# Feed-forward units of seven products: deferring the seventh, exchanging the fifth and sixth

## The chip, the cores and the metric

The kernel runs on one core of a Trainium2 chip. The metric is device time in microseconds for one execution, taken over several executions; the median of the runs is used. A profile of one execution gives each engine's instructions with their times. Engines: TensorE (PE) multiplies, ScalarE (ACT), VectorE (DVE) and GpSimd (POOL) work on tiles, SyncE (SP) issues the transfers.

## The reference

One decoder block on x of 2048 positions by 1024 channels, float32, batch 1:

```
h  = rmsnorm(x); z = h @ w_in                    # one combined input projection
a  = gated linear attention on part of z          # 4 heads, in chunks of 64
b  = B * conv3(C * h') on the rest of z           # causal, width 3
x1 = x + concat(a, b) @ w_out
f  = rmsnorm(x1); y = x1 + (silu(f @ w_gate) * (f @ w_up)) @ w_down   # D_FF = 2816
out = rmsnorm(y)
```

The change concerns the last matrix products, those with w_gate, w_up and w_down.

## The kernel before, in words

Tensors lie with channels on the 128 partitions and positions in the free dimension, in blocks of 512 positions (PB). The positions are worked on in two halves of two blocks each.

**A unit.** Every large product is cut into units. A unit multiplies a 2x2 arrangement of weight blocks by a 2x2 arrangement of operand blocks with seven products in place of eight (PRODUCTS, L36 to 39): A11·B11, S1·T1, S2·T2, A12·B21, S3·T3, S4·B22, A22·T4. The S are sums of weight blocks, made on POOL in `unit_weights` (L424 to 441: L430, L431, L432, and L437 for S4's, which overwrites A12's raw block). The T are sums of operand blocks, made ahead. A product adds the partial products of its blocks of 128 channels in one PSUM bank; it is 12 matmuls in the input projection and in the gate and up products (four blocks), 9 in most down products (three), 6 in the first group of them (two). Each block takes three matmuls (`product_step`, L443 to 450), since weights and operands are split into a high and a low part: `split` (L162) rounds with ACT (L163) and subtracts with DVE (L164). Split weights lie in a pool of four buffers (`wqp`), split operands in a pool of 28 (`opp`).

**Evacuation.** The seven products of a unit use two banks, `oa` and `ob` (L483 to 497). A11 goes to `oa`, which ACT copies to c11 (L480); S1 goes to `ob`, copied to c22; S2 is accumulated on top of A11 in `oa`, copied to c12; A12 goes to a bank of its own and DVE adds it to c11 (`plus`, L472 to 473); S3 is accumulated in `oa`, which DVE adds to c22; S4 is accumulated in `ob`, which DVE adds to c12; A22 is accumulated in `oa`, which is c21. So S2 may begin when c11 is copied, S3 when c12 is copied, S4 when c22 is copied, and A22 when `oa` has been added to c22. In down units of a later group the copies are DVE adds onto the running sums y (`onto`); in the first group they are ACT copies to y (`into`).

**Feed-forward.** `ffn_up` (L1048) goes through 11 pairs of units for each half: an even unit gives gate values, which ACT puts through silu (L512), an odd unit gives the factor, which DVE multiplies in (L1054). POOL then makes T1 to T4 for the down product (L1058), and `split_later` (L1065) splits and stores them in the background. `ffn_down` (L1083) takes them in groups starting at 0, 2, 5 and 8 (GROUPS), four units in each. The last unit of half 1 is `last_unit` (L1162). `load_pairs` (L662) and `load_h2` (L1039) load a whole half's operands; LATER (L42) is the order in which `h2_rest` (L995) splits the later operands of half 0.

**Work beside it.** During half 0's first units `h2_ahead` (L1022) prepares half 1's operands: `position_rstd` (L187) sums squares with small matmuls (`rs`, L196), does Newton steps on tiles of 128x4 on DVE (L200, L213 to 218), spreads the result (`rep`, L204) and turns it with PE (`rb_ps`, L208). `finish_later` does the like for the final norm of half 0's output during half 1.

**What sets the order.** The whole kernel is one program in a tile framework that tracks the readiness of tiles and is asked to schedule by a simulated timeline (L1383). The order in which an engine gets its instructions is that scheduler's. The source order is a priority, `issue_after` and `behind` (L155) add constraints, and each engine then runs its own stream in order.

Of the kernel before, what the change touches and what calls it, by code (L numbers as in the profile page):

```python
# [19 lines left out]
P = 128  # L20
D = 1024
SEQ = 2048
PB = 512
# [17 lines left out]

LATER = ("B21", "T3", "B22", "T4")  # L42

# [9 lines left out]
def tile_hymba_block(ctx, tc, x, xt, win, wa, wgu, wout, wffn, wdown, wdown_first, small, out):  # L53
# [93 lines left out]
    def store(dst, src):  # L147
        return nc.sync.dma_start(dst, src)
# [274 lines left out]

    def unit_weights(src, raw=None):  # L424
        raw = raw_weights(src) if raw is None else raw
        n = src.shape[-1]
        a11, a12, a22, a21 = [raw[:, i, :] for i in range(4)]
        s1 = rawp.tile([P, PB], F32, name="s1", tag="s1", bufs=1)[:, 0:n]
        w = {"A11": weight_quarter(a11)}
        pool.tensor_tensor(s1, a21, a22, ALU.add)  # L430
        pool.tensor_tensor(a21, a11, a21, ALU.subtract)  # L431
        pool.tensor_tensor(a11, s1, a11, ALU.subtract)  # L432
        w["S1"] = weight_quarter(s1)
        w["S2"] = weight_quarter(a11)
        w["A12"] = weight_quarter(a12)
        w["S3"] = weight_quarter(a21)
        pool.tensor_tensor(a12, a12, a11, ALU.subtract)  # L437
# [13 lines left out]

    def unit(src, ops, into=None, onto=None, raw=None):

        w = unit_weights(src, raw)
        unit_splits[:] = last_hi + last_lo
# [4 lines left out]

        def mul(i, o=None):
            first = o is None
            o = bank() if first else o
            n, m = PRODUCTS[i]
# [9 lines left out]
        def copied(name, o, at):  # L476
# [4 lines left out]
            return t  # L481


        oa = mul(0)
        c11 = copied("c11", oa, (0, 0))
        ob = mul(1)
# [12 lines left out]

# [162 lines left out]
    def load_pairs(src):  # L662
        ops = no_operands()
        for _, n in PRODUCTS:
            ops[n] = [(load_whole if n in WHOLE else load_pair)(p) for p in src[n]]
        return ops

    def load_whole(src):
# [80 lines left out]
    def in_proj(half, ops, first=None, differences=None):  # L749
        def units():  # L750
            for u in range(12):
                with ExitStack() as stack:
                    if half == 0 and u == 1:
                        stack.enter_context(tc.issue_after(last_load[0].ins))
                    if half or u > 1:
                        us = unit(win[u], ops)
                    else:
                        us = plain_unit(win[u], ops, differences) if u else first
                if half == 0 and u == 1:
                    del ops["B12"]  # L760
                    differences(("T4",))
                yield us

        units = units()
        for dst, i0 in ((s_kq, 0), (s_kq, 2), (s_v, 0), (s_v, 2)):
            for r, j, c, p in next(units):
                store(dst[2 * half + j][i0 + r][:], settled(c, p)[:])
        for i0 in (0, 2):
            for r, j, c, p in next(units):
                store(s_g[2 * half + j][i0 + r][:], silu(c, p)[:])  # L770
        background.append(gla_half(half))
        for i0 in (0, 2):
            cc = {(r, j): settled(c, p) for r, j, c, p in next(units)}
            ch = {(r, j): c for r, j, c, _ in next(units)}
            for r in range(2):
                i = i0 + r
                left = halo[:, i, :]
                for j in range(2):
                    s = tp.tile([P, PB + 2], F32, name="u", tag="t")
                    dve.tensor_tensor(s[:, 2:], ch[r, j][:], cc[r, j][:], ALU.mult)  # L780
                    act.activation(s[:, 0:2], left, AF.Copy)
                    left = s[:, PB : PB + 2]
                    y = cc[r, j]
                    act.activation(y[:], s[:, 0:PB], AF.Copy, scale=col(C_CW + i))
                    for n in (1, 2):
                        dve.scalar_tensor_tensor(
                            y[:], s[:, n : n + PB], col(C_CW + 4 * n + i), y[:], ALU.mult, ALU.add
                        )
                if half == 0:
                    act.activation(halo[:, i, :], left, AF.Copy)  # L790
            for r, j, c, _ in next(units):
                y = cc[r, j]
# [5 lines left out]
                store(dst[:, 1, :], y[:])  # L798


    def gla_half(half):
# [237 lines left out]
    def load_h2():  # L1039
        ops, loads = no_operands(), raw_loads[-2]  # L1040
        for _, n in PRODUCTS:
            for k in range(4):
                with tc.issue_after(loads.ins):
                    o = (load_whole if n in WHOLE else load_pair)(s_h2p[n][k])
                ops[n].append(o)
        return ops

    def ffn_up(half, ops):  # L1048
        for m in range(NF // 2):
            us = unit(wffn[2 * m], ops)  # L1050
            sg = {(r, j): silu(c, p) for r, j, c, p in us}
            for r, j, c, _ in unit(wffn[2 * m + 1], ops):
                s = sg[r, j]
                dve.tensor_tensor(s[:], c[:], s[:], ALU.mult)  # L1054
            b11, b12, b21, b22 = [sg[r, j] for r in range(2) for j in range(2)]
            t1, t2, t3, t4 = [bt(n) for n in ("t1", "t2", "t3", "t4")]
            for y, p, q in ((t1, b12, b11), (t2, b22, t1), (t3, b22, b12), (t4, b21, t2)):
                pool.tensor_tensor(y[:], p[:], q[:], ALU.subtract)  # L1058
            values = [("B11", b11), ("B21", b21), ("B22", b22)]
            if half == 1 and m >= LAST_GROUP:  # L1060
                values.append(("B12", b12))
            values += [("T1", t1), ("T2", t2), ("T3", t3), ("T4", t4)]
            background.insert(0, split_later(s_act[half][m], values))

# [15 lines left out]
    def act_op(half, m, n):  # L1080
        return (load_whole if n in WHOLE else load_pair)(s_act[half][m][n])

    def ffn_down(half):  # L1083

# [5 lines left out]
        for u, m0 in enumerate(GROUPS):  # L1090
            ms = range(m0, m0 + (3 if u else 2))
            last = m0 == LAST_GROUP
            if last:
                drain_background()
            raw = None
            if u:
                raw = raw_weights(wdown[4 * u - 4])
                with tc.issue_after(raw_loads[-1].ins):
                    ops = {n: [group_op(m, n) for m in ms] for _, n in PRODUCTS}
            else:  # L1100
                ops = {n: [group_op(m, n) for m in ms] for _, n in PRODUCTS}
            if last and half:
# [4 lines left out]
            for d0 in range(0, KD, 2):  # L1107
                src = wdown[4 * u - 4 + d0 // 2] if u else wdown_first[d0 // 2]
                if u == 0 and d0 == 2:

                    order = [(m, n) for _, n in PRODUCTS for m in range(GROUPS[1], GROUPS[2])]
                    for m, n in order[:EARLY]:
                        early[m, n] = act_op(half, m, n)
                if u == 0:
                    for d in (d0, d0 + 1):
                        if d < KD - 1:
                            pair = opp.tile([P, 2, PB], F32, name="y", tag="op")
                        for j in range(2):
                            y[d, j] = pair[:, j, :] if d < KD - 1 else bt("y")[:]
                    unit(src, ops, {(r, j): y[d0 + r, j] for r in range(2) for j in range(2)})  # L1120
                    continue
                xs = []
                if u < 3:
                    for d in (d0, d0 + 1):
                        xs.append((y[d, u - 1], bt("x1")))
                        load(xs[-1][1][:], s_x1[2 * half + u - 1][d][:])
# [4 lines left out]
                unit(src, ops, onto=onto, raw=None if d0 else raw)  # L1131
                for r, j in ((0, 0), (1, 1), (0, 1), (1, 0)):
                    yy = onto[r, j]
# [3 lines left out]
                    elif last:  # L1137
                        store(s_x1[2 * half + j][d0 + r][:], yy)
                for yy, x1 in xs:
                    pool.tensor_tensor(yy, x1[:], yy, ALU.add)  # L1140
        if half == 0:
# [246 lines left out]
```

## Time and profile before

| quantity | value |
|---|---|
| median of 3 runs | 2062.14 us (2060.34 to 2063.09) |
| span of the profiled execution | 2059.3 us (its own time is not listed apart from it) |
| PE busy | 2018.4 us, 98% |
| DVE, ACT, POOL busy | 69%, 47%, 42% |
| mean granted TensorE clock | 0.996 |

The input projection and the mixers run up to some 570 us, the output projection and what belongs to it up to some 760 us, the feed-forward part from there to the end. In the rows of a timeline or a group, a line such as L473 is that of the kernel before; the name before the arrow is the tile written, the names behind it are those read, with buffer numbers left out; a bracket holds the idle time of the engine ahead of the instruction and what ended it.

### The profile page before, as it was taken

The page shows a single profiled execution, that of the slowest core. Times are in us where ns is not written, and L with a number is a line of the kernel's source. Part 1 is how long each engine was busy: PE and PEld are TensorE (multiplying, and loading weights), DVE is VectorE, ACT ScalarE, POOL GpSimd, SP SyncE. Part 2 cuts the span into 40 slices and gives each one's busy share as a digit, 9 for nine tenths or more (in the row PEclk, how much of TensorE's full clock was granted, in tenths as well). Part 3 has the DMA queues.
Part 4 walks back from the last instruction along what each step waited for, and adds up shares of the span by engine and source line. Part 5 has one row for each costly group of instructions (what it writes and reads, how often), then busy time and mean ns, then how long its engine had stood idle before and what let it go on. Part 6 is the DMA issues. An engine that isn't in the chain of part 4 may idle for free.

```text
span 2059.3 us, 27063 instructions
## 1 busy us (share of the span) xinstructions
PE 2018.4 (98%) x9229; PEld 1657.3 (80%) x9229; DVE 1425.3 (69%) x2128; ACT 959.7 (47%) x1918; POOL 859.8 (42%) x622
## 2 busy tenths in 40 slices
PE   7999999999999999999999999999999999999997
PEld 6877888787888888888888878787888888878786
DVE  8789686559743886676675676767666666667774
ACT  6655365765542344444444452334434444453344
POOL 0345322122102564464564345534644544435544
PEclk9999999999999999999999999999999999999998
DMA  6378485416586873545454676476444434586653
GB/s 229 116 274 278 159 319 165 143 67 194 190 296 246 311 254 130 198 181 207 156 185 143 241 264 254 185 282 257 163 164 167 175 140 169 179 309 223 234 217 126
DMA packets 188729, 421.47 MB, mean 205 GB/s; under 512 B 19792, under 2 KB 65072, under 8 KB 178992
## 3 DMA queue, kind: packets, MB, share of 16 engines
q1 hardware_dynamic: 188592, 419.76, 57.2%
q8 instruction: 72, 1.18, 0.2%
q14 instruction: 65, 0.53, 0.1%
HBM read 274.98 MB, written 144.70 MB: 204 GB/s over the span
## 4 chain that ended last, share of the span: by engine, by line
PE 84%; DVE 7%; DMA 4%; ACT 3%; issue 1%; POOL 1%; SPq 0%; DVEq 0%; ACTq 0%; POOLq 0%
PE mm L448 24%; PE mm L449 23%; PE mm L450 23%; PE mm L945 3%; PE mm L948 3%; PE mm L946 3%; DVE wq L164 2%; DVE op L164 1%; DMA op<-sa_B 1%; DMA op<-sa_T 1%; PE a_ps L702 1%; ACT wq L163 1%; DMA siT<-lo 1%; PE o_ps L869 1%; PE o_ps L871 1%
## 5 line engine op out<-in xcount | busy, mean ns | idle before, releaser
L448 PE MATMUL mm<-op,wq 128*128 128x512 f32 x2499 | 973.7, 392 | 10.3 <-ACT c L480 5.3
L449 PE MATMUL mm<-op,wq 128*128 128x512 f32 x2499 | 972.5, 390 | 1.6 <-DVE op L164 1.6
L450 PE MATMUL mm<-op,wq 128*128 128x512 f32 x2499 | 961.3, 390 | 2.6 <-DVE wq L164 2.3
L164 DVE TENSOR_TENSOR wq<-raw,wq 128x512 fp32r<-128x512 f32 (+2 forms) x626 | 508.9, 818 | 262.6 <-ACT wq L163 260.0
L163 ACT ACTIVATE wq<-raw 128x512 fp32r<-128x512 f32 (+2 forms) x626 | 364.9, 589 | 585.6 <-PE mm L450 447.9
L448 PEld LDWEIGHTS mm<-op,wq 128*128 128x128 f32 x2499 | 468.9, 188 | 114.9 <-ACT c L480 8.0
L450 PEld LDWEIGHTS mm<-op,wq 128*128 128x128 f32 x2499 | 469.1, 188 | 103.8 <-DVE wq L164 6.1
L449 PEld LDWEIGHTS mm<-op,wq 128*128 128x128 f32 x2499 | 469.3, 188 | 99.1 <-DVE op L164 3.7
L432 POOL TENSOR_TENSOR raw<-s,raw 128x512 f32<-128x512 f32 (+2 forms) x97 | 133.3, 1374 | 518.5 <-DVE wq L164 474.7
L430 POOL TENSOR_TENSOR s<-raw 128x512 f32<-128x512 f32 (+2 forms) x97 | 127.4, 1313 | 247.5 <-DMA raw<-in_wffn_dram 90.7
L473 DVE TENSOR_TENSOR c<-mm,c 128x512 f32<-128x512 f32 x198 | 135.8, 686 | 72.7 <-PE mm L450 70.9
L473 DVE TENSOR_TENSOR y<-mm,y 128x512 f32<-128x512 f32 x185 | 126.9, 687 | 83.3 <-PE mm L450 82.9
L437 POOL TENSOR_TENSOR raw<-raw 128x512 f32<-128x512 f32 (+2 forms) x97 | 120.6, 1244 | 126.7 <-DVE wq L164 126.7
L927 POOL TENSOR_TENSOR ssx<-ssx,q 128x512 f32<-128x512 f32 x52 | 77.4, 1504 | 158.8 <-ACT q L926 158.5
L431 POOL TENSOR_TENSOR raw<-raw 128x512 f32<-128x512 f32 (+2 forms) x97 | 137.3, 1416 | 4.9
L480 ACT ACTIVATE c<-mm 128x512 f32<-128x512 f32 x198 | 116.1, 587 | 11.1 <-PE mm L450 9.3
L945 PE MATMUL mm<-op,wq 128*128 128x512 f32 x256 | 100.9, 395 | 0.0
L946 PE MATMUL mm<-op,wq 128*128 128x512 f32 x256 | 99.7, 389 | 0.0
L163 ACT ACTIVATE wq<-s 128x512 fp32r<-128x512 f32 (+2 forms) x97 | 56.9, 587 | 89.3 <-PE mm L450 85.4
L164 DVE TENSOR_TENSOR wq<-s,wq 128x512 fp32r<-128x512 f32 (+2 forms) x97 | 82.6, 852 | 2.8 <-ACT wq L163 2.1
L164 DVE TENSOR_TENSOR op<-op 128x512 fp32r<-128x512 f32 x94 | 76.8, 844 | 4.7 <-ACT op L163 4.6
L948 PE MATMUL mm<-op,wq 128*128 128x512 f32 x256 | 79.8, 390 | 0.0
(204 smaller groups left out, 1807.6 us busy)
## 6 DMA issues: line engine op xcount, KB each, us to landing
raw<-in_wffn_dram SPq DMA_DIRECT2D x44, 1024.0 KB, 6.5
sa_B<-so SPq DMA_DIRECT2D x47, 512.0 KB, 4.2
op<-sa_B SPq DMA_DIRECT2D x47, 512.0 KB, 7.1
raw<-in_win_dram SPq DMA_DIRECT2D x23, 1024.0 KB, 5.4
sa_T<-so SPq DMA_DIRECT2D x44, 512.0 KB, 4.5
op<-sa_T SPq DMA_DIRECT2D x44, 512.0 KB, 6.9
raw<-in_wdown_dram SPq DMA_DIRECT2D x24, 768.0 KB, 5.8
sx<-y SPq DMA_DIRECT2D x48, 256.0 KB, 4.0
```

Source lines behind the costliest of these rows:

```text
L163: last_hi[:] = [act.activation(hi, src, AF.Copy)]
L164: last_lo[:] = [dve.tensor_tensor(lo, src, hi.bitcast(F32), ALU.subtract)]
L430: pool.tensor_tensor(s1, a21, a22, ALU.add)
L431: pool.tensor_tensor(a21, a11, a21, ALU.subtract)
L432: pool.tensor_tensor(a11, s1, a11, ALU.subtract)
L448: pe.matmul(o[:], wh, xh, start=first and k == 0, stop=False, skip_group_check=True)
L449: pe.matmul(o[:], wh, xl, start=False, stop=False, skip_group_check=True)
L450: return pe.matmul(o[:], wl, xh, start=False, stop=k == n - 1, skip_group_check=True)
L473: dve.tensor_tensor(t[:], o[:], t[:], ALU.add)
L945: pe.matmul(o[e, j][:], wh, m[:, 0, :], start=k == 0, stop=False)
L946: pe.matmul(o[e, j][:], wh, m[:, 1, :], start=False, stop=False)
L948: pe.matmul(o[e, j][:], wl, ops[k][j][:, 0, :], start=False, stop=k == KD - 1)
```

## The change

In the feed-forward units the source now puts the seventh product A22 behind the next unit's A11 and S1 (`pending`, `rest`, `fourth`), and S4 ahead of S3. Each unit's weights are split in that order (S4 ahead of S3). The operands T4 of the next stage are loaded only when the deferred product has been written (`late`, `fill_now_or_late`). Since c21 now comes later, a unit no longer returns its results: it hands each to a function `use` (`gated`, `raised` in `gate_and_up`, which replaces the body of `ffn_up`). The input projection keeps its old order (`close=True`), as does the last but one down unit of half 1; `in_proj` is rewritten to the form with `use`, and the convolution becomes a function. LATER takes B22 ahead of T3, and the orders of loading take OVERLAPPED.

The core of the diff:

```diff
+OVERLAPPED = [PRODUCTS[i] for i in (0, 1, 2, 3, 5, 4, 6)]
-LATER = ("B21", "T3", "B22", "T4")
+LATER = ("B21", "B22", "T3", "T4")
...
-    def unit_weights(src, raw=None):
+    pending, late, operand = [], [], dict(PRODUCTS)
+
+    def unit_weights(src, raw, close):
...
-        w["S3"] = weight_quarter(a21)
+        if close:
+            w["S3"] = weight_quarter(a21)
         pool.tensor_tensor(a12, a12, a11, ALU.subtract)
         w["S4"] = weight_quarter(a12)
+        if not close:
+            w["S3"] = weight_quarter(a21)
         w["A22"] = weight_quarter(a22)
...
+        def rest():
+            mul("A22", oa)
+            if into is not None or onto is not None:
+                copied("c21", oa, (1, 0))
+            return oa
+
+        def fourth():
+            rest()
+            if use is not None:
+                use(1, 0, oa, True)
+
+        oa = mul("A11")
         c11 = copied("c11", oa, (0, 0))
+        ob = mul("S1")
         c22 = copied("c22", ob, (1, 1))
-        mul(2, oa)
+        if before is not None:
+            before()
+        while late:
+            late.pop(0)()
+        mul("S2", oa)
         c12 = copied("c12", oa, (0, 1))
-        plus(c11, mul(3))
-        mul(4, oa)
-        plus(c22, oa)
-        mul(5, ob)
+        plus(c11, mul("A12"))
+        if close:
+            mul("S3", oa)
+            plus(c22, oa)
+        mul("S4", ob)
         plus(c12, ob)
-        mul(6, oa)
-        if into is not None or onto is not None:
-            copied("c21", oa, (1, 0))
-        return [(0, 0, c11, False), (1, 1, c22, False), (0, 1, c12, False), (1, 0, oa, True)]
+        if not close:
+            mul("S3", oa)
+            plus(c22, oa)
+        if close:
+            rest()
+        if use is not None:
+            for r, j, c in ((0, 0, c11), (1, 1, c22), (0, 1, c12)):
+                use(r, j, c, False)
+            if close:
+                use(1, 0, oa, True)
+        if not close:
+            pending.append(fourth)
...
+    def fill_now_or_late(n, fill):
+        if n == PRODUCTS[-1][1] and pending:
+            late.append(fill)
+        else:
+            fill()
...
+                close = bool(last and half and d0 == KD - 4)
+                unit(src, ops, use, onto=onto, raw=None if d0 else raw, close=close)
```

More of the change, by code (lines that the diff above doesn't have):

```diff
@@ L450, in product_step, with unit @@
         return pe.matmul(o[:], wl, xh, start=False, stop=k == n - 1, skip_group_check=True)
-    def unit(src, ops, into=None, onto=None, raw=None):
-        w = unit_weights(src, raw)
+    def unit(src, ops, use=None, into=None, onto=None, raw=None, close=False):
+        w = unit_weights(src, raw, close)
+        before = pending.pop() if pending else None
         unit_splits[:] = last_hi + last_lo
@@ L749, in in_proj @@
     def in_proj(half, ops, first=None, differences=None):
[L750 to L767, printed above, removed]
+        count = iter(range(12))
+        def run(use):
+            u = next(count)
+            if half or u > 1:
+                unit(win[u], ops, use, close=True)
+                return
+            us = first
+            if u:
+                with tc.issue_after(last_load[0].ins):
+                    us = plain_unit(win[u], ops, differences)
+                del ops["B12"]
+                differences(("T4",))
+            for x in us:
+                use(*x)
@@ L768, in in_proj, with keep, output_gate @@
+        for s, i0 in ((s_kq, 0), (s_kq, 2), (s_v, 0), (s_v, 2)):
+            def keep(r, j, c, p, s=s, i0=i0):
+                store(s[2 * half + j][i0 + r][:], settled(c, p)[:])
+            run(keep)
         for i0 in (0, 2):
-            for r, j, c, p in next(units):
+            def output_gate(r, j, c, p, i0=i0):
                 store(s_g[2 * half + j][i0 + r][:], silu(c, p)[:])
-        background.append(gla_half(half))
+                if (i0, r, j) == (2, 1, 0):
+                    background.append(gla_half(half))
+            run(output_gate)
@@ L772, in in_proj @@
         for i0 in (0, 2):
[L773 to L790, printed above, removed]
@@ L791, in in_proj, with first_factor, second_factor, output_factor @@
-            for r, j, c, _ in next(units):
+            cc, ch = {}, {}
+            def first_factor(r, j, c, p, cc=cc):
+                cc[r, j] = settled(c, p)
+            def second_factor(r, j, c, p, cc=cc, ch=ch, i0=i0):
+                ch[r, j] = c
+                if (r, 1 - j) in ch:
+                    convolution(half, i0 + r, [ch[r, e] for e in range(2)], [cc[r, e] for e in range(2)])
+            def output_factor(r, j, c, p, cc=cc, i0=i0):
                 y = cc[r, j]
@@ L798, in in_proj, with convolution @@
                 store(dst[:, 1, :], y[:])
+            for use in (first_factor, second_factor, output_factor):
+                run(use)
+    def convolution(half, i, ch, cc):
+        left = halo[:, i, :]
+        for j in range(2):
+            s = tp.tile([P, PB + 2], F32, name="u", tag="t")
+            dve.tensor_tensor(s[:, 2:], ch[j][:], cc[j][:], ALU.mult)
+            act.activation(s[:, 0:2], left, AF.Copy)
+            left = s[:, PB : PB + 2]
+            y = cc[j]
+            act.activation(y[:], s[:, 0:PB], AF.Copy, scale=col(C_CW + i))
+            for n in (1, 2):
+                dve.scalar_tensor_tensor(
+                    y[:], s[:, n : n + PB], col(C_CW + 4 * n + i), y[:], ALU.mult, ALU.add
+                )
+        if half == 0:
+            act.activation(halo[:, i, :], left, AF.Copy)
     def gla_half(half):
@@ L1040, in load_h2, with fill @@
         ops, loads = no_operands(), raw_loads[-2]
[L1041 to L1045, printed above, removed]
+        for _, n in OVERLAPPED:
+            def fill(n=n):
+                for k in range(4):
+                    with tc.issue_after(loads.ins):
+                        o = (load_whole if n in WHOLE else load_pair)(s_h2p[n][k])
+                    ops[n].append(o)
+            fill_now_or_late(n, fill)
         return ops
@@ L1081, in act_op, with group_ops, fill @@
         return (load_whole if n in WHOLE else load_pair)(s_act[half][m][n])
+    def group_ops(ms, group_op, marks):
+        ops = no_operands()
+        for _, n in OVERLAPPED:
+            def fill(n=n):
+                with behind(marks):
+                    ops[n] += [group_op(m, n) for m in ms]
+            fill_now_or_late(n, fill)
+        return ops
     def ffn_down(half):
@@ L1094, in ffn_down @@
                 drain_background()
[L1095 to L1101, printed above, removed]
+            raw = raw_weights(wdown[4 * u - 4]) if u else None
+            ops = group_ops(ms, group_op, raw_loads[-1:] if u else [])
             if last and half:
@@ L1109, in ffn_down @@
                 if u == 0 and d0 == 2:
-                    order = [(m, n) for _, n in PRODUCTS for m in range(GROUPS[1], GROUPS[2])]
+                    order = [(m, n) for _, n in OVERLAPPED for m in range(GROUPS[1], GROUPS[2])]
                     for m, n in order[:EARLY]:
@@ L1119, in ffn_down @@
                             y[d, j] = pair[:, j, :] if d < KD - 1 else bt("y")[:]
[L1120 removed]
+                    unit(src, ops, into={(r, j): y[d0 + r, j] for r in range(2) for j in range(2)})
                     continue
[L1122 removed]
+                xs = {}
                 if u < 3:
[L1124 to L1126 removed]
+                    for r in range(2):
+                        x1 = xs[r, u - 1] = bt("x1")
+                        load(x1[:], s_x1[2 * half + u - 1][d0 + r][:])
                 if last and half and d0 == KD - 2:
@@ L1130, in ffn_down, with use @@
                 onto = {(r, j): y[d0 + r, j] for r in range(2) for j in range(2)}
-                unit(src, ops, onto=onto, raw=None if d0 else raw)
-                for r, j in ((0, 0), (1, 1), (0, 1), (1, 0)):
+                def use(r, j, *_, onto=onto, xs=xs, last=last, d0=d0):
                     yy = onto[r, j]
```

53 lines of the change are left out of this document (32 added, 21 removed).

## The prediction

> **What bounds the kernel now.** I first read the busy shares and the granted clock on the page, then the busy time by stretch from 760 us on (the feed-forward part), then the waits of PE there.
>
> ```profile
> span 2059.3 us, 27063 instructions
> PE 2018.4 (98%) x9229; PEld 1657.3 (80%) x9229; DVE 1425.3 (69%) x2128; ACT 959.7 (47%) x1918; POOL 859.8 (42%) x622
> PEclk9999999999999999999999999999999999999998
> ...
> 850.00:950.00 100.00, 100.00 (x443) 82.78 (x442) 67.50 (x86) 46.85 (x83) 48.12 (x34) 1.00 0.52 185
> ...
> 1050.00:1150.00 100.00, 100.00 (x443) 82.81 (x442) 59.62 (x75) 41.82 (x73) 49.55 (x36) 1.00 0.41 146
> ```
>
> PE is the bound. In the 300 us from 850 to 1150 (the first and last of three rows alike are shown) it is busy without a break at clock 1.00: 443 matmuls in 100 us, 0.226 us each, so a product of 12 matmuls is 2.72 us and a unit of seven 19.0 us. In such a stretch no order of products can gain anything; only a wait of PE can be taken away. These are all of PE's waits from 760 us to the end (waited for: us in total, times, longest):
>
> ```profile
> PE mm L448 <- ACT c L480: 3.5, 3, 1.7
> PE mm L448 <- DVE y L473: 3.4, 3, 1.7
> PE rb_ps L1195 <- DVE rep L1188: 1.7, 1, 1.7
> PE mm L449 <- DVE op L164: 1.6, 2, 1.4
> PE rs L1175 <- ACT q L1232: 1.4, 1, 1.4
> PE rb_ps L208 <- DVE rep L204: 0.9, 1, 0.9
> PE mm L450 <- DVE wq L164: 0.5, 2, 0.3
> PE mm L448 <- DVE c L473: 0.4, 1, 0.4
> ```
>
> They sum to 13.4 us, of which 3.1 (L1195, L1175) belong to the end of the kernel, behind the last product. So the whole feed-forward part offers about 10 us, 0.5% of the time.
>
> **What the change really moves.** The source of before runs a unit's seven products and then the next unit's. The chip does not: the kernel is built with a list scheduler (L1383), and the profile shows what that made of it. This is DVE in one up-projection unit (start us, us, engine, line):
>
> ```profile
> 911.65 0.69 DVE L473 TENSOR_TENSOR c<-mm,c 128x512 f32<-128x512 f32 x1 [0.19 <-PE mm L450]
> ...
> 914.37 0.69 DVE L473 TENSOR_TENSOR c<-mm,c 128x512 f32<-128x512 f32 x1 [0.33 <-PE mm L450]
> ...
> 922.31 0.69 DVE L1054 TENSOR_TENSOR sg<-mm,sg 128x512 f32<-128x512 f32 x1 [3.08 <-PE mm L450]
> ```
>
> The first two add the fifth and sixth products in the order run; the third reads the seventh from PSUM. It comes 922.31 − 914.37 = 7.94 us after the sixth, three products, not one: two products of the next unit already stand between. The built instruction streams say the same by name. Before runs, in its usual unit, A11', S1' (11 of 12 matmuls), A22 of the unit before, A12' and S2' mixed, S4', S3': the deferral and the exchange that the diff writes down are there. After runs A11', S1', A22, A12' and S2' mixed, S4', S3'. Both streams hold the same number of instructions on every engine and the same order on each up to about 765 us. I therefore cost the change only where the two orders differ at a wait. Below, H0u3 is unit 3 (from 0) of half 0's up-projection; even units are gates.
>
> **Removed.** Four places of before wait for an evacuation that after issues earlier, or further from its reader.
>
> ```profile
> 833.55 0.39 PE L450 MATMUL mm<-op,wq 128*128 128x512 f32 x1
> 833.95 0.63 ACT L163 ACTIVATE so<-c 128x512 fp32r<-128x512 f32 x1 [2.76 <-DVE c L1054]
> 834.49 0.58 ACT L480 ACTIVATE c<-mm 128x512 f32<-128x512 f32 x1
> 835.12 0.50 PE L448 MATMUL mm<-op,wq 128*128 128x512 f32 x1 [1.18 <-ACT c L480]
> 835.46 0.40 PE L449 MATMUL mm<-op,wq 128*128 128x512 f32 x1
> ...
> 1425.64 0.39 PE L450 MATMUL mm<-op,wq 128*128 128x512 f32 x1
> 1427.08 0.59 ACT L480 ACTIVATE c<-mm 128x512 f32<-128x512 f32 x1
> 1427.72 0.50 PE L448 MATMUL mm<-op,wq 128*128 128x512 f32 x1 [1.70 <-ACT c L480]
> ...
> 1501.31 0.95 PE L196 MATMUL rs<-ones,ssx 128*128 128x1 f32 x8
> 1502.29 0.59 ACT L480 ACTIVATE c<-mm 128x512 f32<-128x512 f32 x1
> 1502.93 0.50 PE L448 MATMUL mm<-op,wq 128*128 128x512 f32 x1 [0.67 <-ACT c L480]
> ...
> 1686.00 0.40 PE L450 MATMUL mm<-op,wq 128*128 128x512 f32 x1
> 1686.23 0.50 PE L196 MATMUL rs<-ones,ssx 128*128 128x1 f32 x4
> 1686.43 0.69 DVE L473 TENSOR_TENSOR c<-mm,c 128x512 f32<-128x512 f32 x1 [0.94 <-PE mm L450]
> 1687.18 0.50 PE L448 MATMUL mm<-op,wq 128*128 128x512 f32 x1 [0.44 <-DVE c L473]
> ```
>
> A wait costs its start-to-start time less 0.23, and 0.11 more for the matmul behind it (835.46 − 835.12 = 0.34, not 0.23).
> - H0u3, product S3: 835.12 − 833.55 − 0.23 + 0.11 = **1.45**. The copy of c12, which frees the bank, stood on ACT behind a split of `so` that waited for DVE's gate product. In after the copy is ahead of that split. What is late next is nothing nearer than the 13 matmuls between.
> - H1u1, S2: 1427.72 − 1425.64 − 0.23 + 0.11 = **1.96**, for the copy of c11. In after the first unit's products end earlier beside the second's, and the copy is issued before S1'.
> - H1u5, S2: 1502.93 − 1502.26 (the end of the eight `rs` matmuls) + 0.11 = **0.8**; in after A22 of the unit before stands between, 12 matmuls for a copy of 0.59.
> - H1u14, A22 directly behind its own S3: 0.44 + 0.11 = **0.6**, and the wait for `rep` behind it (L204, the row of 0.9 above, + 0.11) **1.0**. In after H1u15's A11 and the `rs` matmuls stand between.
>
> Sum **−5.8** (−4.3 if H0u3's stays).
>
> **Added.** In two units after puts A22 directly behind its own S3, where before had two products of the next unit between: H0u1 and H0u2. There h2_ahead's row statistics (position_rstd) stand in DVE's queue, and the next unit's weight splits with them. PE then waits for `plus(c22)`. Its floor is what H1u14 shows with an idle DVE: 1687.18 − 1686.00 − 0.23 + 0.11 = 1.06 us, twice 2.1. To it comes what is queued on DVE ahead of that add. In H0u1 this is, during S4 and S3 (5.4 us): two weight splits, one split of `so`, two gate products (L1054), the add of c12 and nine or ten Newton steps. Before runs the same kind of work a little elsewhere:
>
> ```profile
> 789.01 0.68 DVE L1054 TENSOR_TENSOR c<-c,c 128x512 f32<-128x512 f32 x1
> 789.61 0.17 DVE L213 TENSOR_SCALAR rs<-rs 128x4 int32<-128x4 int32 x1
> 789.81 0.16 DVE L214 TENSOR_SCALAR py<-rs 128x4 int32<-128x4 int32 x1
> ...
> 797.47 1.51 DVE L164 TENSOR_TENSOR wq<-raw,wq 128x512 fp32r<-128x512 f32 x1
> 798.90 1.77 DVE L1054 TENSOR_TENSOR c<-c,c 128x512 f32<-128x512 f32 x1
> ...
> L164 DVE TENSOR_TENSOR wq<-raw,wq 128x512 fp32r<-128x512 f32 x436 | 382.9, 883 | 239.7 <-ACT wq L163 237.1
> ...
> L473 DVE TENSOR_TENSOR c<-mm,c 128x512 f32<-128x512 f32 x198 | 135.8, 686 | 72.7 <-PE mm L450 70.9
> ```
>
> At 0.2 us a Newton step (789.81 − 789.61) and 0.69 the rest, that is 10 × 0.2 + 6 × 0.69 = 6.1 us in 5.4: 0.7 late. At 1.51 and 1.77 for half of the five that slow down (beside POOL) it is about 3 late. I take 0.9, near the fast rows at 789 us, as POOL mostly waits in that stretch: 2.0 for H0u1 (1.06 to 4.1). H0u2 has one split less and no gate product: 1.4 (1.06 to 3.0). `rb` (L208) then follows A22 and waits for a `rep` whose chain passes the same queue: 0.3 (0 to 1.2). Sum **+3.7** (2.1 to 8.3).
>
> A rule of the Trainium skill speaks against this place. By "SBUF — State Buffer", section "SBUF: two separate sides", a DVE instruction with two SBUF inputs and a GpSimd one that reads SBUF exclude each other for a whole instruction, whichever begins first. The trace agrees: splits and gate products (two SBUF inputs) run 0.68 or up to 1.77, the adds out of PSUM 0.686 on average over 198. By that rule, if POOL works through the whole stretch, the two waits would be the upper ends above and the sum +2.5; by what I take it is −2.1.
>
> **Costed at nothing.** The waits at the first down units (1197 and 1839 us, DVE y, 1.5 to 1.7 each), at 1289 to 1305, 1409 and 1931 to 1947 have the same queue ahead of them in both streams, so I leave them: between −1 each and +1. The S3/S4 exchange of the weights puts S4's split on ACT ahead of S3's, where it waits for POOL's L437 (rivals). T4's later loads are the same transfers on the same queue, read by the seventh product, over two products away. LATER only reorders splits. New tight places (S3 directly behind S4 in some down units; A12's split) have covers of 1.4 us against a copy of 0.59: 0 to 0.5 each, taken as 0.
>
> **Sum.** −5.8 + 3.7 = −2.1 on the profiled span: 2059.3 → 2057.2. The median of the three runs lies 2.84 above that span (the execution's own time is not given apart from it), so **2062.1 − 2.1 = 2060.0 us**.
>
> **Rivals.**
> 1. *Slower: S4's weights come late in every unit.* The chain is A12's split, L437 on POOL, S4's split, with ACT's queue held at its head meanwhile. For it: ACT waits for L437 in before already. Rows:
>
> ```profile
> ACT wq L163 <- POOL raw L437: 36.8, 21, 4.5
> ...
> L437 POOL TENSOR_TENSOR raw<-raw 128x512 f32<-128x512 f32 x66 | 89.3, 1354 | 89.8 <-DVE wq L164 89.8
> ```
>
> Against it: from the release of A12's buffer to S4's first matmul lie 49 matmuls in both streams, 11.1 us; the chain is 0.63 + 1.77 + 1.35 + 0.63 + 1.77 = 6.2, or 8.9 with two more POOL instructions of that length ahead. It decides once it passes 11.1 us. If it did so by 0.3 in each of the 44 up units: +13.2 beside the −2.1, 2073 us; from half of them on it is 2066.6, slower than before by over 0.2%.
> 2. *Faster: the written order frees more than I list.* If the waits that I left alone also go (3.4 + 1.6 + 0.5 = 5.5), or DVE is not late at H0u1 and H0u2 (2.1 in place of 3.7): −3.7 to −9, 2053 to 2058.4. For it: these waits stem from the same kind of queueing. Against: the two streams agree there.
> 3. *No change beyond noise, because the old order was already the new one.* This is my forecast; if not even the four waits go, but the added ones come, +3.7: 2066.
>
> **How the numbers follow.** A measurement of this kernel can tell about 0.2% (4.1 us) from no change: faster is under 2058.0, slower over 2066.3. Chances: the forecast 0.60 (own range 2058 to 2066), the faster rival 0.22, the slower rival with the upper ends of the added waits 0.18. So faster 0.22, same 0.60, slower 0.18. For 8 in 10 the range takes the forecast's range and the nearer part of the faster rival: 2056 to 2066.5.
>
> **What would show it right or wrong.** In the profile of after: PE's waits for ACT's c copy fall from 3.5 to under 1; a wait for DVE's c add (the line of `plus`) rises from 0.4 to 2 to 6, in two pieces between 780 and 820 us; 850 to 1150 stays at 100 busy in every 100 us; the y waits stay near 3.4. It is wrong if gaps appear in the steady stretch, above all waits for wq (rival 1), if the c-add wait stays under 1, or if the y waits go.

## The result, and the profile after

After takes 2066.47 us (median of 6 runs, 2065.95 to 2071.88), before 2061.07 (median of 6, 2059.01 to 2063.09): ratio **1.0027, 95% interval 1.0015 to 1.0039**, slower by 5.4 us. The forecast was 2060.0, 2.1 us faster than before. The time lies at the very upper end of the range, 2056 to 2066.5; the sign is wrong.

The page of after, and all of PE's waits from 760 us on (waited for: us in total, times, longest; line numbers in the rows from here on are those of the kernel they come from; in after L456 to L458 are the three matmuls of product_step, L482 is `plus`, L489 the ACT copy, L166 and L167 the two halves of `split`):

```profile
span 2065.0 us, 27060 instructions
PE 2021.9 (98%) x9229; PEld 1657.5 (80%) x9229; DVE 1401.8 (68%) x2128; ACT 959.8 (46%) x1918; POOL 861.1 (42%) x622
...
PE mm L458 <- DVE wq L167: 7.4, 10, 1.3
PE mm L456 <- DVE y L482: 2.4, 2, 1.3
PE rb_ps L1274 <- DVE rep L1267: 1.7, 1, 1.7
PE mm L456 <- DVE c L482: 1.6, 2, 0.8
PE rs L1254 <- ACT q L1311: 1.4, 1, 1.4
PE rb_ps L211 <- DVE rep L207: 1.0, 1, 1.0
```

The waits for ACT's copies of c (3.5 in before) are gone, and so are those for `op` (1.6). The two directly following seventh products show as the wait for DVE's c, 1.6. What is new and large is the first row: PE waits ten times, 7.4 us, for the low half of split weights; before had 0.5. Part of it lies where before had no gap at all (busy by stretch):

```profile
850.00:950.00 100.00, 99.60 (x439) 81.91 (x438) 61.66 (x83) 46.05 (x82) 51.15 (x36) 1.00 0.51 179
950.00:1050.00 100.00, 99.55 (x438) 81.86 (x437) 66.45 (x85) 43.80 (x77) 56.47 (x38) 1.00 0.51 180
1050.00:1150.00 100.00, 98.81 (x436) 81.38 (x435) 61.52 (x78) 43.65 (x75) 46.56 (x33) 1.00 0.44 157
```

DVE is less busy in them than before (189.6 us in 300 against 199.5), so it is no want of DVE time: the splits stand at another place in its queue.

**Where the time went.** Both kernels have the same number of product matmuls, so the n-th of one can be laid beside the n-th of the other, and the difference of their start times followed. This is by how much it grows in each stretch (us; times are those of before):

| stretch of before | forecast | after | what it is |
|---|---|---|---|
| to 774 | 0 | +1.92 | there by 600 us, where both streams are alike; see the last section |
| 774 to 820 | +3.7 | +3.39 | H0u1 and H0u2, seventh directly behind sixth |
| 820 to 838 | −1.45 | −1.40 | H0u3, copy of c12 |
| 838 to 1172 | 0 | **+3.36** | A11 of H0u7 and u11, S1 of u15 split late |
| 1172 to 1285 | 0 | −0.33 | first down groups |
| 1285 to 1405 | 0 | **+2.31** | last down group of half 0 |
| 1405 to 1440 | −1.96 | −3.31 | H1u1's c11, and the wait for `op` at 1410 |
| 1440 to 1700 | −2.4 | −2.23 | H1u5, H1u14 |
| 1700 to 2036 | 0 | **+2.02** | down units of half 1, most in the last group |

From 774 us on this is +3.8. The three bold rows, which the forecast put at nothing, are 7.7 together.

The added seventh products look as they were drawn. In H0u2 (start, us, engine, line):

```profile
821.07 0.39 PE L458 MATMUL mm<-op,wq 128*128 128x512 f32 x1
...
821.49 0.69 DVE L482 TENSOR_TENSOR c<-mm,c 128x512 f32<-128x512 f32 x1 [0.30 <-PE mm L458]
...
822.24 0.50 PE L456 MATMUL mm<-op,wq 128*128 128x512 f32 x1 [0.78 <-DVE c L482]
```

DVE was idle for 0.30 before the add: the queue that the forecast feared had run empty, and the wait is the bare floor, 822.24 − 821.07 − 0.23 + 0.11 = 1.05. H0u1 has the same 0.78. The rest of the 3.39 is mostly `rb` behind H0u1's, which waited 1.05 for `rep`.

The late A11 split, H0u7, in after:

```profile
893.85 0.63 ACT L166 ACTIVATE wq<-raw 128x512 fp32r<-128x512 f32 x1 [0.62 <-ACT so L166]
...
894.10 1.39 DVE L647 SCALAR_TENSOR_TENSOR h<-h,sml,rb_ps 128x512 f32<-128x512 f32 x2
895.41 1.40 DVE L167 TENSOR_TENSOR wq<-raw,wq 128x512 fp32r<-128x512 f32 x1
896.74 0.74 DVE L647 SCALAR_TENSOR_TENSOR h<-h,sml,rb_ps 128x512 f32<-128x512 f32 x1
897.40 0.68 DVE L167 TENSOR_TENSOR so<-t,so 128x512 fp32r<-128x512 f32 x1
898.00 0.68 DVE L482 TENSOR_TENSOR c<-mm,c 128x512 f32<-128x512 f32 x1
898.60 1.40 DVE L167 TENSOR_TENSOR wq<-raw,wq 128x512 fp32r<-128x512 f32 x1
...
898.16 1.29 POOL L310 TENSOR_TENSOR t<-h,t 128x512 f32<-128x512 f32 x1 [1.89 <-DVE so L167]
...
899.27 0.39 PE L457 MATMUL mm<-op,wq 128*128 128x512 f32 x1
900.05 0.50 PE L458 MATMUL mm<-op,wq 128*128 128x512 f32 x1 [0.40 <-DVE wq L167]
```

ACT has A11's high half at 894.48. DVE comes to the low half only at 898.60, after scalings of h and a split of `so` that belong to h2_ahead, and then takes 1.40 in place of 0.68, with POOL at work beside it on L310, which is h2_ahead's too. (That fits the Trainium skill, "SBUF — State Buffer", section "SBUF: two separate sides": such a DVE instruction and a reading GpSimd one shut each other out for a whole instruction. No run here took POOL's part away alone.) PE needs the low half 0.55 us earlier than it comes. The same place in before:

```profile
889.94 0.64 ACT L163 ACTIVATE wq<-raw 128x512 fp32r<-128x512 f32 x1 [1.36 <-issue]
...
894.40 0.67 DVE L164 TENSOR_TENSOR wq<-raw,wq 128x512 fp32r<-128x512 f32 x1
...
895.59 0.39 PE L450 MATMUL mm<-op,wq 128*128 128x512 f32 x1
```

There the split ended at 895.07, 0.52 us ahead of its matmul. The margin was half a microsecond in before already. It was readable from that trace, and the forecast did not read it.

The two sets of rows also show what used it up. DVE begins 3.82 us after the end of ACT's half in before (890.58) and 4.12 in after, so its queue costs 0.30; the slower run of the split itself costs 0.73, and in before POOL was idle beside it. The split is slow at the other two places too: those of u11 and u15 took 1.41 and 1.38 in after, beside L310 and L319 of h2_ahead, and 0.67 and 0.68 in before. An estimate from these rows: at 0.68 the first two would have come in time (0.72 and 0.73 saved, for 0.55 and 0.60 late), and S1 of u15 would still have been 0.65 of its 1.35 late, for its place in the queue.

### The profile page after: what moved, and what is told of

Its sections match the earlier page's. It is cut to its first block, busy times and chain, and to the rows that moved or that the text cites. A ratio compares the mean times of both kernels' runs of the same rounds, so it can differ in the third digit from the quotient of the medians.

```text
span 2065.0 us, 27060 instructions
## 1 busy us (share of the span) xinstructions
PE 2021.9 (98%) x9229; PEld 1657.5 (80%) x9229; DVE 1401.8 (68%) x2128; ACT 959.8 (46%) x1918; POOL 861.1 (42%) x622
## 4 chain that ended last, share of the span: by engine, by line
PE 80%; DVE 8%; DMA 5%; ACT 3%; issue 2%; POOL 1%; SPq 1%; DVEq 0%; ACTq 0%; POOLq 0%
PE mm L456 23%; PE mm L458 23%; PE mm L457 22%; PE mm L999 2%; PE mm L1000 2%; PE mm L1002 2%; DVE wq L167 2%; DVE op L167 2%; ACT wq L166 1%; PE a_ps L742 1%; DMA op<-sa_B 1%; DVE h L647 1%; DMA h<-in_xt_dram 1%; DVE so L167 1%; PE o_ps L923 1%
## 5 line engine op out<-in xcount | busy, mean ns | idle before, releaser
L456 PE MATMUL mm<-op,wq 128*128 128x512 f32 x2499 | 972.1, 393 | 6.7 <-DVE y L482 2.4
L458 PE MATMUL mm<-op,wq 128*128 128x512 f32 x2499 | 968.5, 391 | 8.9 <-DVE wq L167 8.8
L167 DVE TENSOR_TENSOR wq<-raw,wq 128x512 fp32r<-128x512 f32 (+2 forms) x626 | 483.1, 778 | 342.2 <-ACT wq L166 339.4
L166 ACT ACTIVATE wq<-raw 128x512 fp32r<-128x512 f32 (+2 forms) x626 | 361.3, 587 | 620.8 <-PE mm L458 372.8
L458 PEld LDWEIGHTS mm<-op,wq 128*128 128x128 f32 x2499 | 469.3, 188 | 114.2 <-DVE wq L167 16.3
L456 PEld LDWEIGHTS mm<-op,wq 128*128 128x128 f32 x2499 | 469.4, 188 | 109.7 <-DVE y L482 3.8
L437 POOL TENSOR_TENSOR raw<-s,raw 128x512 f32<-128x512 f32 (+2 forms) x97 | 138.5, 1428 | 500.8 <-DVE wq L167 471.8
L482 DVE TENSOR_TENSOR c<-mm,c 128x512 f32<-128x512 f32 x198 | 135.6, 685 | 81.5 <-PE mm L458 79.5
L482 DVE TENSOR_TENSOR y<-mm,y 128x512 f32<-128x512 f32 x185 | 126.6, 686 | 79.8 <-PE mm L458 76.3
L489 ACT ACTIVATE c<-mm 128x512 f32<-128x512 f32 x198 | 115.8, 586 | 71.4 <-PE mm L458 67.6
L166 ACT ACTIVATE wq<-s 128x512 fp32r<-128x512 f32 (+2 forms) x97 | 56.6, 583 | 60.2 <-PE mm L458 51.9
L167 DVE TENSOR_TENSOR op<-op 128x512 fp32r<-128x512 f32 x94 | 80.4, 881 | 2.9 <-ACT op L166 2.9
L167 DVE TENSOR_TENSOR wq<-s,wq 128x512 fp32r<-128x512 f32 (+2 forms) x97 | 76.4, 787 | 3.4 <-ACT wq L166 3.2
```

The costliest lines, as they stand in the source:

```text
L166: last_hi[:] = [act.activation(hi, src, AF.Copy)]
L167: last_lo[:] = [dve.tensor_tensor(lo, src, hi.bitcast(F32), ALU.subtract)]
L456: pe.matmul(o[:], wh, xh, start=first and k == 0, stop=False, skip_group_check=True)
L458: return pe.matmul(o[:], wl, xh, start=False, stop=k == n - 1, skip_group_check=True)
L482: dve.tensor_tensor(t[:], o[:], t[:], ALU.add)
```

## The experiments

The forecast's sum having failed at waits for split weights, **theory A** was that these come with the new source order of the products (deferral and exchange), in half 0 and at the last down groups alike; **rival B** that they come from other parts of the diff; **rival C** that every new built order has some such waits by chance. Four kernels undo the order in parts; `close=True` writes a unit in the old order.

```diff
-        unit(wffn[2 * m], ops, gated)
+        unit(wffn[2 * m], ops, gated, close=half == 0)
-        unit(wffn[2 * m + 1], ops, raised)
+        unit(wffn[2 * m + 1], ops, raised, close=half == 0)
-                    unit(src, ops, into={(r, j): y[d0 + r, j] for r in range(2) for j in range(2)})
+                    unit(src, ops, into={(r, j): y[d0 + r, j] for r in range(2) for j in range(2)}, close=True)
-                close = bool(last and half and d0 == KD - 4)
+                close = True
```

The second run has the first two pairs of lines, the fourth the last two, the third all four, and the first all four with `close=True` in both halves.

**All units in the old order.** 

> Every feed-forward unit is written in the old order again (close for all), while the callbacks, the operand loading orders and the new LATER stay. Theory A (the loss sits where the new source order changes the built streams: two seventh products directly behind their sixth in half 0, and weight splits that come late on DVE): as before, ratio to before 0.999 to 1.001, PE's waits for wq from 760 us on back to about 0.5 us. Rival B (the loss comes from the other parts of the diff: later T4 loads, LATER, loading order): still 1.002 to 1.003, waits for wq still about 7 us.

Measured: 1.0022 (1.0013 to 1.0031). Theory A fails here. Half 0's up units are as in before (0.0 from 774 to 1172 us), but of after's losses at the last groups +1.79 (1285 to 1405) and +1.50 (1920 to 1958) stay, with the old order written everywhere. They belong to something else in the diff: rival B, for this part. The new LATER, which this kernel keeps, costs half 0's up units nothing.

**Half 0's up units old.** 

> Only the 22 up-projection units of half 0 are written in the old order; the rest is as in after. Theory A: about 5 us less than after (the two seventh products 3.4, the late A11 and S1 splits of 900 to 1058 us 3.1, less 1.2 for the wait at unit 3 that comes back), so ratio 1.000 to 1.001; no gap between 850 and 1150 us. Rival C (late splits are a matter of chance in each built order and not of the deferral in half 0): gaps of 1 to 3 us turn up elsewhere and the ratio stays at 1.002 or above.

Measured: 1.0006 (0.9997 to 1.0015), and no wait between 850 and 1150 us. Half 0's loss is from the new order there; +2.55 at the last group stays. Between 1172 and 1285 us this kernel loses 1.75, where after gained 0.33; no run settles why.

**Only half 1's up units new.** 

> Old order in half 0's up units and in all down units; only half 1's 22 up units are written in the new order. Theory A: it keeps the gains of half 1 (1410, 1428, 1503 and 1687 us, about 5.5 us) and has neither half 0's losses nor those at the last down groups (about 2 each): 2061 - 5 = about 2056, ratio 0.997 to 0.998, faster than both kernels. Rival B or C: within 0.1% of before or slower.

Measured: 1.0001 (0.9993 to 1.0010), a miss by 5 us. The gains of half 1 are there (−3.82 from 1405 to 1700 us), and the last groups take them back (+2.09, +1.51).

**Down units old.** 

> Only the down units are written in the old order; all up units are new. Theory A: the waits for wq at the last group of each half (unit 63 at 1298 to 1310 us and unit 101 at 1945 to 1949 us in after, about 2 us more each than in before) go, half 0's losses stay: about 3 to 4 us less than after, ratio 1.0005 to 1.0015. Rival C: no fall, 1.002 to 1.003, with the same waits at new places.

Measured: 1.0032 (1.0022 to 1.0043), a miss: with the down units in the old order the waits at units 63 and 101 are the same to 0.1 us.

So the loss at the last groups does not hang on the order of the products. The built streams name another part. `group_ops` loads a group's operands in the order OVERLAPPED, B22 ahead of T3. With that the scheduler puts the seventh product of the last group's first unit (unit 62 of the stream; 100 in half 1) behind the whole A12 of the next one; with PRODUCTS it puts eight of its matmuls between A12's second and third. **Theory A2**: that loading order is the cause. For half 0, **theory D**: h2_ahead takes a step every fourth product, seven steps to a round, 28 products, four units; the late splits come every four units; so the loss is a meeting of its steps with the new order. **Rival E**: the deferral makes A11's split late, whatever runs beside it.

**The loading order undone in after.**

```diff
     def group_ops(ms, group_op, marks):
-        for _, n in OVERLAPPED:
+        for _, n in PRODUCTS:
...
-                    order = [(m, n) for _, n in OVERLAPPED for m in range(GROUPS[1], GROUPS[2])]
+                    order = [(m, n) for _, n in PRODUCTS for m in range(GROUPS[1], GROUPS[2])]
```

> The kernel after, but the operands of the down groups are loaded in the order of PRODUCTS again (T3 ahead of B22), nothing else. Theory A2 (new: what is lost at the last group of each half comes from the loading order, since with B22's operands first the scheduler puts the seventh product of unit 62 and of unit 100 behind the next unit's whole A12, and A12's split on DVE, queued behind operand splits, is then waited for with nothing between): the waits of 1.5 us at A12 of units 63 and 101 and about 0.5 more at each go, 4 us less than after, ratio 1.0005 to 1.0015; half 0's losses up to 1060 us stay as in after. Rival C (chance): the same sum of waits at other places.

Measured: 1.0000 (0.9991 to 1.0009), a little below the expected range. From 1285 to 1405 us it is −0.43 in place of +2.31, from 1920 us on −0.37 in place of +1.72; half 0 is as in after (+3.43, −1.40, +3.39). PE's wait for weights between 1280 and 1320 us falls from 2.5 to this:

```profile
PE mm L458 <- DVE wq L167: 0.4, 2, 0.3
```

**The same with only half 1's up units new.** 

> Old order in half 0's up units and all down units, the down groups' operands loaded in the old order, only half 1's up units in the new order. Theory A2: as the third run (ratio 1.0001) less 3.5 to 4 us at units 63 and 101: 2057 to 2058, ratio 0.998 to 0.9985, faster than both kernels. Rival C: 1.000.

Measured: 0.9985 (0.9977 to 0.9994), faster than both kernels.

**The work ahead two products later.**

```diff
-        elif ahead and pace[0] % 4 == 1:
+        elif ahead and pace[0] % 4 == 3:
```

> The kernel after, but the work ahead for half 1's operands takes its steps two products later (at the third of four ticks in place of the first); all products and splits as in after. Theory D (the losses in half 0 come from where the steps of that work fall beside the new order: the two seventh products behind their sixth, and A11 and S1 split late once in four units, which is one round of seven steps of it): they go or move to other units, the sum from 760 to 1190 us changes by several us, most likely down by 3 to 5. Rival E (the deferral itself makes A11's split late, whatever runs beside it): waits for wq at 900, 977 and 1058 us stay.

Measured: 0.9998 (0.9989 to 1.0008). Half 0's up units are now 0.84 us faster than before, where after was 5.35 slower, with the same products, splits and deferral. Busy by stretch of this kernel:

```profile
850.00:950.00 100.00, 100.00 (x442) 82.79 (x442) 62.27 (x84) 45.90 (x80) 49.50 (x33) 1.00 0.51 182
...
1050.00:1150.00 100.00, 100.00 (x443) 82.81 (x442) 56.24 (x74) 42.46 (x74) 50.13 (x35) 1.00 0.38 142
```

Neither the late splits nor the two directly following seventh products are left. The last groups lose as in after, and half 1 gives up 2.2 between 1440 and 1518 us (+1.35 in place of −0.80); finish_later takes its steps at the shifted products there, which was not tried apart.

**The work ahead behind half 0's up units.**

```diff
-        elif ahead and pace[0] % 4 == 1:
+        elif ahead and late_ahead and pace[0] % 4 == 1:
...
         ffn_up(half, load_h2() if half else h2)
+        if half == 0:
+            for _ in ahead[0]:
+                pass
+            late_ahead.append(True)
```

> The kernel after, but the work ahead for half 1's operands is issued after half 0's up units and not beside them (all of it is still done). Theory D: no wait of PE between 760 and 1150 us, all at full pace; the cost comes back between 1170 and 1300 us, where that work meets the down units. Rival E: waits for wq remain between 850 and 1150 us.

Measured, one run: 2092.19. Half 0's up units run without a gap:

```profile
850.00:950.00 100.00, 100.00 (x443) 82.81 (x442) 56.15 (x75) 42.59 (x73) 43.71 (x30) 1.00 0.38 138
950.00:1050.00 100.00, 100.00 (x443) 82.81 (x442) 58.66 (x74) 44.02 (x75) 49.02 (x34) 1.00 0.37 137
1050.00:1150.00 100.00, 100.00 (x443) 82.81 (x442) 55.49 (x71) 41.62 (x71) 49.11 (x33) 1.00 0.33 121
```

Between 1172 and 1285 us it then loses 31.8 us, where that work meets the down units (part of it at a lower granted clock, 0.93 from 1150 to 1300 us). Theory D holds and rival E falls: without the work ahead, or with it two products later, the deferral makes no split late.

**The loading order alone, in before.**

```diff
-                    ops = {n: [group_op(m, n) for m in ms] for _, n in PRODUCTS}
+                    ops = {n: [group_op(m, n) for m in ms] for _, n in OVERLAPPED}
...
-                    order = [(m, n) for _, n in PRODUCTS for m in range(GROUPS[1], GROUPS[2])]
+                    order = [(m, n) for _, n in OVERLAPPED for m in range(GROUPS[1], GROUPS[2])]
```

> The kernel before with one part of the change alone: the operands of the down groups are loaded in the new order (B22 ahead of T3); no deferral, no exchange. Theory A2 (this order alone makes the loss at the last group of each half): the same 1.5 us at A12 of units 63 and 101 and about 0.5 more at each, 3.5 to 4 us more than before, ratio 1.0013 to 1.0022; 760 to 1190 us as in before. Rival B2 (the loading order costs only together with the new order of the products): ratio 1.000.

Measured: 1.0016 (1.0006 to 1.0025). No unit is deferred in its source, and the loss is there. This kernel at A12 of unit 63:

```profile
1300.64 0.39 PE L451 MATMUL mm<-op,wq 128*128 128x512 f32 x1
1302.38 0.50 PE L452 MATMUL mm<-op,wq 128*128 128x512 f32 x1 [1.35 <-DVE wq L166]
...
1301.78 0.54 DVE L166 TENSOR_TENSOR wq<-raw,wq 128x384 fp32r<-128x384 f32 x1
```

and before:

```profile
1301.85 0.54 DVE L164 TENSOR_TENSOR wq<-raw,wq 128x384 fp32r<-128x384 f32 x1
...
1302.52 0.62 PE L450 MATMUL mm<-op,wq 128*128 128x512 f32 x2
```

The split comes at the same time in both, to 0.07 us. In before eight matmuls of the other unit's seventh product, 1.8 us, stand ahead of the matmul that reads it (the second of the last row); here they don't. What changed is the cover, not the split.

**The two halves of the change alone.** The exchange without the deferral:

```diff
-        if close:
-            rest()
+        rest()
...
-            if close:
-                use(1, 0, oa, True)
-        if not close:
-            pending.append(fourth)
+            use(1, 0, oa, True)
```

> The kernel after without the deferral: the seventh product is written at its unit's end again, S4 stays ahead of S3. Theory D (half 0's losses come from where the work ahead falls, and any change of the source order moves that): losses in half 0 of another size at other places, one seventh product directly behind its sixth (unit 34 of the stream, 1 to 2 us); half 1's wait at 1687 us, which hangs on the deferral, stays. Rival F (the deferral alone makes the losses): none of half 0's.

The deferral without the exchange, the splits of the weights in the old order too:

```diff
-        if close:
-            mul("S3", oa)
-            plus(c22, oa)
+        mul("S3", oa)
+        plus(c22, oa)
         mul("S4", ob)
         plus(c12, ob)
-        if not close:
-            mul("S3", oa)
-            plus(c22, oa)
```

> The kernel after without the exchange: products and splits in the order S3, S4, the seventh product deferred as in after. Theory D: one seventh product directly behind its sixth (unit 33), late splits in half 0 of about the size in after or moved; half 1's waits at 1428, 1503 and 1687 us gone as in after. Rival F: all of half 0's losses of after, the same size at the same places.

Measured, one run each, so without an interval: 2064.42 and 2062.93, before 2061.03. From 774 to 1172 us the exchange alone gives +1.29: one seventh product directly behind its sixth (wait 0.8) and small waits of 0.3 for copies at other units, no late A11. The deferral alone gives +1.48: −1.51 at H0u3 and +2.97 from the same late splits as in after at the same units. So rival F is right that the late splits come with the deferral, and wrong that nothing else is needed (seventh run). The exchange alone brings one of the two directly following products, the deferral alone none that PE waits for (in the one expected, at unit 33, six matmuls of S4 stand between S3 and it), so the two waits need both parts. Rival F's other side, no loss in half 0 without the deferral, fails with the +1.29. Of half 1's gains, 1428, 1503 and 1687 us go with the deferral (−4.32 from 1405 to 1700 us); the exchange alone gains 1.4 there. The deferral alone has a wait of its own, 1.0 us for S4's high half at 1395 us, which no theory here named.

**Both repairs.** After with the old loading order of the fifth run, and the work ahead two products later in half 0 alone:

```diff
-        elif ahead and pace[0] % 4 == 1:
+        elif ahead and pace[0] % 4 == (1 if second else 3):
...
         ffn_up(half, load_h2() if half else h2)
+        second.append(half)
```

> The kernel after with two repairs: the down groups' operands loaded in the old order (as in the fifth run, 4 us), and the work ahead two ticks later in half 0 alone (as in the seventh, about 5 us), half 1 as in after. Theory A2 + D: the sum of both, about 9 us less than after and 3.5 to 5 less than before: ratio 0.9975 to 0.9985; no wait for wq over 0.2 us between 850 and 1150 us. Rival C (each new built order has as many waits elsewhere): 1.000 or above.

Measured: **0.9973 (0.9963 to 0.9983)**, 2055.57 against 2061.03: the fastest of all, and a little below the expected range. Its page and its waits from 760 us on:

```profile
span 2053.7 us, 27061 instructions
...
PE mm L457 <- DVE y L483: 2.4, 2, 1.2
PE rb_ps L1275 <- DVE rep L1268: 1.7, 1, 1.7
PE rs L1255 <- ACT q L1312: 1.4, 1, 1.4
PE mm L459 <- DVE wq L167: 1.1, 3, 0.6
PE rb_ps L211 <- DVE rep L207: 0.8, 2, 0.4
PE mm L458 <- DVE op L167: 0.4, 1, 0.4
```

Waits for weights are 1.1 in place of 7.4. Rival C in its general form falls with this run: the new order need not lose elsewhere what it gains. That single builds bring waits of their own (the second run's 1.75, the deferral alone) is not excluded.

## Why the prediction was wrong

- *PE is the bound and only its waits can be gained* held, and so did *the new order is there already*: in every kernel tried, whichever way the source was written, a usual unit was built in the same order, A11, S1, A12 and S2 mixed, S4, S3, A22 two products on.
- *Removed, −5.8.* Right, −5.6. H0u3 −1.40 for 1.45, H1u1 −2.0 for 1.96, H1u5 and H1u14 together −2.23 for 2.4. The wait at 1410 us went too, −1.3, where I had left it.
- *Added, +3.7.* Right in size, +3.39, not in its make-up: DVE was not late for the adds (1.05 each, the floor), and the wait for `rep` took what I gave to DVE, 1.2 with its after-effect. So the size was luck in part. (My +2.5 for POOL at work throughout also takes the upper end of `rb`; with the two adds alone it is +1.6.)
- *Costed at nothing* is the step that failed, twice. In half 0 the fault lies in the rule *cost the change only where the two orders differ at a wait*: for the splits of A11 and S1 before had no wait, so the forecast gave them no term and no reason. Their low half is made by DVE, in its queue's order, and at H0u7 the margin was 0.52 us in before. The queue and POOL beside the splits used up more than that, which cost 3.36 in half 0. And I wrote of the last groups *the same queue ahead of them in both streams*: true of A12's split, which came at the same time in before with the new loading order, but the matmuls that stood between it and PE were moved by that order. It cost 2.3 and about 2 us. *A12's split … 0 to 0.5 each* was 1.5 each.
- *Rival 1* named the right kind of wait, weights late, at the wrong product. In after PE never waits for S4's weights: all ten waits are at A11, S1, S2 and A12, so the 11.1 us of cover held. I gave slower 0.18 because I priced that rival by S4 alone.
- By the forecast's own steps: −5.8 came as −5.6, +3.7 as +3.4, 0 as +6.0 (with the −1.3 at 1410 us); sum +3.8 from 774 us on, against −2.1. The medians' 5.4 has an interval of 3.1 to 8.0 us, which holds it.

## What to carry to other kernels

Where a scheduler sets the order, a source edit's effect is that of the stream it builds, and parts that look like housekeeping (in what order operands are loaded, at which step background work advances) can cost as much as the edit is worth. To cost such an edit, list for each operand of the bound engine when its last producer really ended and when it was read; a margin under a microsecond is where a new order may have to pay, as 0.52 us did here, whatever the buffer count says. When an edit wins in one stretch and loses in another, undo it by stretch and by part: here a few lines turned +0.27% into −0.27%.

## What the runs showed that was not expected

Before about 730 us all these kernels issue the same instructions in the same order on every engine (SyncE is the first to differ, at 732 us in before, where LATER's new order loads other `h` tiles; the forecast's 765 us holds for the others). Yet at 774 us the profiled executions lie from 1.0 us ahead of before's to 1.9 behind it, nearly all of it already at 600 us. Behind it the places repeat to some hundredths across kernels: the two seventh products gave +3.39, +3.34 and +3.43 in three kernels, A12 of unit 101 +1.47 to +1.49 in every kernel with the new loading order. So an edit of 1 us can be read off a single trace, place by place, where the medians need runs in both kernels by the dozen.
